# Another order of the products where the up projection ends and the down projection begins

## The chip, the cores and the metric

One core of a Trainium2 chip runs the whole layer in one launch. TensorE (PE in the profile) multiplies, with its weight loads as a row of their own (PEld); VectorE (DVE), ScalarE (ACT) and GpSimd (POOL) do the rest; SyncE (SP) and POOL issue the DMAs. The time is that of the device in microseconds (us), the median of several runs. One run was taken with the hardware profiler, and all rows come from it.

## The reference

A hybrid encoder layer on 512 tokens of width 2048, cut to its steps:

```python
# per layer (DEPTH = 1), x: 512 x 2048 float32
h = rms_norm(x, pre_mix_g);  z = h @ w_in            # q, k, v, u
a = chunked_attention(q, k, v, rel_bias)
p = multiscale_pool(u, pool_w, pool_scale)
x = x + rms_norm(concat(a, p) @ w_o, post_mix_g)
h = rms_norm(x, pre_ffn_g)
up = causal_dwconv(h @ w_up, conv_w, conv_b)         # 512 x 11264, three taps and a bias
y = (gelu(up[:, :5632]) * up[:, 5632:]) @ w_down     # 5632 -> 2048
out = x + rms_norm(y, post_ffn_g)
```

What the change touches is the join of the last two products, `h @ w_up` (2048 to 2 x 5632) and the one with `w_down` (5632 to 2048).

## The kernel before

All numbers are float32. Each factor of a product is split into a high part, rounded by ScalarE (L135), and a low part, the rest, by VectorE (L136); `mm3` makes a product of three matmuls, high by high (L153), high by low (L154) and low by high (L155). So each factor costs a ScalarE and a VectorE pass before TensorE can use it, and TensorE meets the high parts first.

Both projections are multiplied in blocks by Winograd's form of Strassen's scheme: seven products of half-size blocks instead of eight, numbered 1 to 7, with sums of blocks as factors and sums of products as results.

**Up projection.** `w_up` is cut into 22 units of 2 x 256 columns; unit u has a gate member and a product member. The first three units (`PLAIN`) are multiplied plainly; the other 19 make 38 members k = 0 to 37, two to a unit, the even one the gate, the odd one the product. Member k has seven products (k, i), each of 24 matmuls `q<-...` with 256 columns. `Factors.order` is the hand-written order of them all; each get of a factor makes the split four products ahead (`AHEAD`), on four pairs of buffers (`w4`), and raw blocks are loaded up to ten ahead (`RAW`). In the ordinary member the order is 4, 1, 2, then 6 of the member before, 5, 7, then 3 of the member before. Block sums of weights are made by accumulating DMAs on POOL's queue (`add`, L997) in the raw buffer that the product before has left: x holds the factor of 4, then of 5, then of 6, and with VectorE's L1003 that of 3; y holds that of 1, then of 7. In a member that is `alone` the factor of 4 has a raw buffer of its own (`w`), and 5 comes first.

The stationary factors of products 4, 7 and 6 are h4, h7 and h6 (`hs`), high and low, in the right-hand buffers raw1, wh and wl; those buffers later hold the first factors of the down projection.

After (k, 6) `keep_six` sums four of the results (L1045 on ScalarE, L1046 to L1051 on VectorE); after (k, 3) `keep_all` adds the rest (L1056), scales (L1057), and then either `gate` (three taps on ScalarE L846 and VectorE L847, L848, and the gelu L860) or `product` (the same taps, two multiplications L867, and a store to `gd` by POOL, L870 or L872).

**Down projection.** Five chunks c of four units each (the last two units come at the end). In a chunk there are seven products for each of two halves of the columns, cc = 0 and 1: (cc, i). Each has 24 matmuls `p<-bh,ah` and so on with 512 columns, made by `multiply`. The left factor `a` comes from `gd` (`gc` in the trace, loaded at L1140), the right one `t` or `b` from `w_down` (L802, L770); in chunk 0 all sums of right blocks are in DRAM already, so each right factor is one load of 1 MB. `ORDER0` is the order of chunk 0. `keep_product` brings a result from PSUM into a `part` buffer, by ScalarE's copy (L832), or, for products 2, 3 and 4 (`ADDED`), by VectorE's addition to the part of product 1, 5 or 7 (L828), in place; POOL stores it to one of the sums in DRAM, or accumulates it there (L837, L839). There are five `part` buffers.

**The passage.** The buffers of the up projection (`big`, `p3`) are closed before those of the down projection (`p4`) open in the same memory. So the first two products of chunk 0 are prepared while the up projection still runs (`next_first`, `first_left`, `rights`), in old buffers, and multiplied right after its last product; the next ones use buffers of p4, whose loads wait until their memory is free. In what follows P1 to P6 are the first six products of chunk 0.

TensorE's order is that of the code (`manual_schedule`). The instructions of all other engines are put in order by a planner from its own estimate of times, the earlier in the code the sooner where it has the choice; on the chip each engine keeps that order. `issue_after` holds P1's and P2's copies behind the splits of P3.

Of the kernel before, what the change touches and what calls it, by code (L numbers as in the profile page):

```python
# [31 lines left out]
CU = 4  # L32
# [13 lines left out]
def f32(ap):  # L46
    return ap.bitcast(F32)
# [28 lines left out]
def encoder_layer(ctx: ExitStack, tc: tile.TileContext, x, xT, vecs, rel, post_mix, post_ffn,  # L76
# [7 lines left out]
    nc = tc.nc  # L84
# [16 lines left out]
    def bank(name):  # L101
        return psum.tile([P, 512], F32, tag="ps", name=name)
# [4 lines left out]
    def raw4(name):  # L107
        return big.tile([P, 1024], F32, tag="raw", bufs=5, name=name)

    def w4(name):  # L110
        return big.tile([P, 1024], F32R, tag="w4", bufs=8, name=name)
# [21 lines left out]
    def split(hi, lo, src, scale=None):  # L133
        if scale is None:
            rounded = nc.scalar.activation(hi, src, AF.Copy)  # L135
            nc.vector.tensor_sub(lo, src, f32(hi))  # L136
        else:
            rounded = nc.scalar.activation(hi, src, AF.Copy, scale=scale)
            nc.vector.scalar_tensor_tensor(lo, src, scale, f32(hi), op0=ALU.mult, op1=ALU.subtract)
        split.last = rounded.ins  # L140
        return rounded.ins
# [23 lines left out]
    def part(w, *idx):  # L165
        return tuple(v[(slice(None),) + idx] for v in w)
# [24 lines left out]
    def qk_specs(h):  # L191
        return halves(f"q{h}", w_in, head_cols("q", h), 8, P), halves(f"k{h}", w_in, head_cols("k", h), 8, P)
# [24 lines left out]
    for h in range(1, HEADS):  # L217
        q, k = qk_specs(h)
# [67 lines left out]
    for kb in range(KD):  # L286
        i, o = divmod(kb, 8)
        nc.sync.dma_start(xt[kb // 4][:, kb % 4, :], xT[kb * P:(kb + 1) * P, :])
        for what in "qk":
            if kb in chunks:  # L290
                raw, hi, lo = first[f"{what}0_{i}"]
# [5 lines left out]
        for what in "qk":  # L297
            _, hi, lo = first[f"{what}0_{i}"]
# [11 lines left out]
    with tc.tile_pool(name="p1", bufs=2, reuse_waits="tile") as p1:  # L310
# [5 lines left out]
        with tc.issue_after(last_split):  # L316
            for kb in range(KD):
                sq = t512("tmp")
                nc.scalar.activation(sq, xt[kb // 4][:, kb % 4, :], AF.Square)
                if kb == 0:  # L320
                    before = sq
                else:
                    nc.gpsimd.tensor_add(ssum, sq, before)
                    before = ssum
# [419 lines left out]
    gd = [[dram.tile([P, CU, 2, H], F32, name=f"gd{c}_{i}") for i in range(2)] for c in range(NC)]  # L744
# [6 lines left out]
    later, turns = {}, {}  # L751

    def right_tile(tag, name, dt=F32R):

        n = turns[tag] = turns.get(tag, -1) + 1
        if later and n % (2 + LATER[tag]) >= 2:
            return later[tag](name, dt)
        return pr.tile([P, CU, S], dt, tag=tag, bufs=2, name=name)
# [3 lines left out]
    def raw1(name, dt=F32):  # L762
        return right_tile("raw1", name, dt)

    def right(c, cc):

        def load(j, l):
            b = later["raw2"](f"b{j}{l}") if j else raw1(f"b{j}{l}")
            r, cs = 256 * CU * c, slice(l * C + cc * S, l * C + (cc + 1) * S)
            nc.sync.dma_start(b, w_down[r:r + 256 * CU, cs].rearrange(  # L770
                "(u j p) n -> p u j n", j=2, p=P)[:, :, j, :])
            return b

        b = {}
        order = yield
        while True:
            i = order
            if c == 0:

                v = first_right(cc, i, raw1 if ORDER0.index((cc, i)) % 5 < 3 else later["raw2"])  # L780
            else:
                for jl in {1: (11, 12), 7: (22,), 2: (21,)}.get(i, ()):
                    b[jl] = load(jl // 10 - 1, jl % 10 - 1)
                if i == 5:
                    nc.vector.tensor_add(b[11], b[11], b[12])  # L785
                if i == 7:
                    nc.vector.tensor_add(b[12], b[22], b[12])
                if i == 6:
                    nc.vector.tensor_add(b[11], b[11], b[22])
                if i == 4:  # L790
                    nc.vector.tensor_add(b[21], b[21], b[11])
                v = b[{1: 11, 5: 11, 7: 12, 6: 11, 2: 21, 3: 22, 4: 21}[i]]
            hi, lo = right_tile("wh", "bh"), right_tile("wl", "bl")
            split(hi, lo, v)
            order = yield hi, lo

    def first_right(cc, i, ring):

        v = ring(f"t{i}")
        source = first_sum[i][cc] if i in first_sum else first_block(cc, *{1: (0, 0), 2: (1, 0), 3: (1, 1)}[i])  # L800
        with tc.issue_after(first_right.last) if first_right.last else nullcontext():
            first_right.last = nc.sync.dma_start(v, source).ins  # L802
        return v
# [4 lines left out]

    LAST = 1, 2, 5, 7, 6, 3, 4

    ORDER0 = ((0, 1), (0, 2), (1, 1), (1, 2), *((cc, i) for i in (5, 6, 3, 7, 4) for cc in range(2)))
    DEST = {1: "16", 5: "57", 7: "57", 6: "16", 2: "11", 3: "53", 4: "74"}
    ADDED = {2: 1, 3: 5, 4: 7}
    kept, begun = {}, set()

    def multiply(l, r):
        ps = [bank(f"p{t}") for t in range(2)]
        for u in range(CU):
            for t in range(2):
                mm3(ps[t], part(l, u, slice(t * P, (t + 1) * P)), part(r, u), u == 0, u == CU - 1)  # L820
        return ps

    def keep_product(c, cc, i, ps):

        if i in ADDED:
            v = kept.pop((cc, ADDED[i]))
            for t in range(2):
                nc.vector.tensor_add(v[:, t, :], ps[t], v[:, t, :])  # L828
        else:
            v = later["part"]("part")  # L830
            for t in range(2):
                nc.scalar.activation(v[:, t, :], ps[t], AF.Copy)  # L832
            kept[cc, i] = v
        n = DEST[i]
        dest = sums[n][:, cc * S:(cc + 1) * S].rearrange("(t p) n -> p t n", p=P)
        if (n, cc) in begun:
            nc.gpsimd.dma_start(dest, v, accum_op=ALU.add)  # L837
        else:
            nc.gpsimd.dma_start(dest, v)  # L839
            begun.add((n, cc))  # L840

    with tc.tile_pool(name="p3", bufs=2, reuse_waits="tile") as p3:
# [116 lines left out]
        class Factors:  # L959
# [3 lines left out]
            def __init__(self):  # L963
                n = 2 * (NU - PLAIN)

                self.order = []
                for k in range(n):
                    late = [(k - 1, 6), (k - 1, 3)] if k else [None] * 2
                    if k in (0, n - 1):
                        o = [(k, 5), (k, 4), (k, 1), (k, 2), late[0], (k, 7), late[1]]  # L970
                    else:
                        o = [(k, 4), (k, 1), (k, 2), late[0], (k, 5), (k, 7), late[1]]
                    self.order += [v for v in o if v]
                self.order += [(n - 1, 6), (n - 1, 3)]
                self.alone = 0, n - 1
                self.raw, self.made, self.loaded, self.used = {}, [], 0, 0

            def block(self, k, m, kh):
# [49 lines left out]
        factors = Factors()  # L1028
# [41 lines left out]

        def first_left():

            def load(i, j):
                v = raw4(f"a{i}{j}").rearrange("p (u n) -> p u n", u=CU)
                nc.sync.dma_start(v, gd[0][i][:, :, j, :])
                return v

            def parts(v):
                hi, lo = (w4(f"a{p}").rearrange("p (u n) -> p u n", u=CU) for p in "hl")
                split(hi, lo, v)  # L1080
                return hi, lo

            for j in range(2):
                yield parts(load(0, j))

        z = up(1, 0, [spread2, lambda: product(0, gate(0, normed(ups[0])), normed(ups[1]))])
        a = gate(1, normed(z))
# [3 lines left out]
        a = gate(2, normed(z))  # L1091
        z = up(2, 1)
        h_difference()
        product(2, a, normed(z))
        rights, lefts, firsts = [right(0, cc) for cc in range(2)], first_left(), []
        for r in rights:
            next(r)
        end = factors.alone[1]

        def next_first():  # L1100

            _, i = ORDER0[len(firsts)]
            r = rights[0].send(i)
            firsts.append((i, next(lefts), r))

        for k, i in factors.order:
            seven(k, i)
            if (k, i) == (end - 1, 3):
                next_first()
            if i == 6:  # L1110
                keep_six(k)
                if k == end:
                    next_first()
            if i == 3:
                keep_all(k)
        firsts = [(i, multiply(l, r)) for i, l, r in firsts]
    phase.close()

    with tc.tile_pool(name="p4", bufs=2, reuse_waits="tile") as p4:
# [46 lines left out]
        def factors():  # L1166
            nonlocal right_split
            for c in range(NC):
# [7 lines left out]
                order = [(cc, i) for cc, o in ((0, ORDER), (1, LAST if c == NC - 1 else ORDER)) for i in o]  # L1176
                for cc, i in order if c else ORDER0[2:]:
                    r = rs[cc].send(i)
# [11 lines left out]
        for f in factors():  # L1190
            ready.append(f)
            if firsts:
                with tc.issue_after(right_split), tc.issue_after(split.last):
                    for i, ps in firsts:
                        keep_product(0, 0, i, ps)
                firsts = ()
            if len(ready) > AHEAD:
                next_product()
# [54 lines left out]
        parts, scaled, ssqs, befores = [[] for _ in range(NT)], [[] for _ in range(NT)], {}, {}  # L1253
# [110 lines left out]
```

## Time and profile before

| what | us |
|---|---|
| median of 3 runs | 1932.14 (1931.54 to 1932.59) |
| the profiled run's own time | 1932.79 |
| its span, first to last instruction | 1931.0 |
| mean granted TensorE clock | 0.996 |

The up projection ends at 1484.95 us of the span, and P1 begins there. How rows are read: "start, duration, engine, line, operation, out<-in" in a timeline, with the idle time before it and what ended that in brackets; in a table of stretches the busy time of each engine, the granted clock, the DMA engines' busy share and GB/s. Buffer numbers are left out of names, so `bl<-t,bh` is any right factor's low part.

### The profile page before, as it was taken

Reading aid. Unit: us, or ns where it says so; the run is one execution under the profiler, and the core shown is the slowest. Engines: PE = TensorE matmul, PEld = TensorE weight load, DVE = VectorE, ACT = ScalarE, POOL = GpSimd, SP = SyncE. Lnnn points to the kernel's source line nnn. Section 1 sums busy time; section 2 is a strip of 40 time slices with the busy share of each in tenths; the row PEclk is TensorE's granted clock in tenths of the full one; section 3 lists DMA queues with packets and bytes.
Section 4 is the critical chain, followed back from the end, with each engine's and each line's share of the span. In section 5 each row is a group of like instructions: output and inputs, shape, how many; then the busy total and the mean of one; then the engine's idle time right before and its main releaser. Section 6 shows DMA issues by size and latency. Waiting matters only on the chain.

```text
span 1931.0 us, 28650 instructions
## 1 busy us (share of the span) xinstructions
PE 1899.8 (98%) x11566; PEld 1707.9 (88%) x11566; DVE 1432.8 (74%) x1618; ACT 915.5 (47%) x1126; POOL 285.3 (15%) x369
## 2 busy tenths in 40 slices
PE   9999999999979999999999999999999899999998
PEld 7888888888868889999999999999999688888886
DVE  5455345587668756887878878788788799998877
ACT  6333233356445434544544445444454655455543
POOL 5110010000010101111111111111110112222221
PEclk9999999999999999999999999999999999999999
DMA  7598395447695957667676676766766999999997
GB/s 244 162 259 217 120 264 142 133 148 250 188 305 184 287 144 162 155 170 188 150 188 157 168 188 150 186 161 166 188 162 196 324 265 250 255 210 240 227 222 238
DMA packets 182789, 386.90 MB, mean 200 GB/s; under 512 B 10944, under 2 KB 62528, under 8 KB 178624
## 3 DMA queue, kind: packets, MB, share of 16 engines
q1 hardware_dynamic: 132704, 249.79, 38.0%
q0 software_dynamic: 49952, 135.28, 37.1%
q8 instruction: 90, 1.47, 0.3%
q14 instruction: 43, 0.35, 0.1%
HBM read 328.40 MB, written 98.57 MB: 221 GB/s over the span
## 4 chain that ended last, share of the span: by engine, by line
PE 92%; DMA 3%; issue 2%; DVE 1%; ACT 1%; SPq 0%; POOL 0%; POOLq 0%; DVEq 0%; ACTq 0%
PE q L154 14%; PE q L153 14%; PE q L155 14%; PE p L155 6%; PE p L153 6%; PE p L154 6%; PE up L154 2%; PE up L155 2%; PE up L153 2%; PE m L153 2%; PE m L154 2%; PE m L155 2%; PE u L153 2%; PE v L153 2%; PE u L154 2%
## 5 line engine op out<-in xcount | busy, mean ns | idle before, releaser
L154 PE MATMUL q<-gTl,wfh 128*128 128x256 f32 x1216 | 344.1, 283 | 0.0
L155 PE MATMUL q<-gTh,wfl 128*128 128x256 f32 x1216 | 344.1, 283 | 0.0
L153 PE MATMUL q<-gTh,wfh 128*128 128x256 f32 x1216 | 344.1, 283 | 0.0
L153 PEld LDWEIGHTS q<-gTh,wfh 128*128 128x128 f32 x1216 | 233.5, 192 | 0.0
L154 PEld LDWEIGHTS q<-gTl,wfh 128*128 128x128 f32 x1216 | 233.5, 192 | 0.0
L155 PEld LDWEIGHTS q<-gTh,wfl 128*128 128x128 f32 x1216 | 233.5, 192 | 0.0
L153 PE MATMUL p<-bh,ah 128*128 128x512 f32 x560 | 219.3, 392 | 4.5 <-ACT ah L135 4.5
L154 PE MATMUL p<-bl,ah 128*128 128x512 f32 x560 | 219.1, 391 | 2.3 <-DVE bl L136 2.3
L155 PE MATMUL p<-bh,al 128*128 128x512 f32 x560 | 219.5, 392 | 1.7 <-DVE al L136 1.7
L135 ACT ACTIVATE wfh<-wx 128x1024 fp32r<-128x1024 f32 x152 | 159.9, 1056 | 119.1 <-PE q L154 91.4
L136 DVE TENSOR_TENSOR wfl<-wx,wfh 128x1024 fp32r<-128x1024 f32 x152 | 183.9, 1220 | 33.5 <-ACT wfh L135 33.4
L135 ACT ACTIVATE wfh<-wy 128x1024 fp32r<-128x1024 f32 x76 | 80.6, 1061 | 119.3 <-PE q L154 105.8
L135 ACT ACTIVATE bh<-b 128x2048 fp32r<-128x2048 f32 x56 | 106.9, 1917 | 61.3 <-DVE b L785 40.6
L136 DVE TENSOR_TENSOR bl<-b,bh 128x2048 fp32r<-128x2048 f32 x56 | 127.7, 2287 | 10.5 <-PE p L154 8.5
L153 PEld LDWEIGHTS p<-bh,ah 128*128 128x128 f32 x560 | 105.8, 189 | 27.1 <-ACT ah L135 5.3
L155 PEld LDWEIGHTS p<-bh,al 128*128 128x128 f32 x560 | 105.9, 189 | 24.8 <-DVE al L136 2.9
L997 POOL DMA_DIRECT2D wx<-in_w_up x76 | 67.5, 888 | 408.3 <-DVE wfl L136 381.5
L154 PEld LDWEIGHTS p<-bl,ah 128*128 128x128 f32 x560 | 105.8, 189 | 24.8 <-DVE bl L136 2.6
L136 DVE TENSOR_TENSOR wfl<-wy,wfh 128x1024 fp32r<-128x1024 f32 x76 | 92.9, 1223 | 32.2 <-ACT wfh L135 30.9
L837 POOL DMA_DIRECT2D sum<-part x60 | 72.7, 1231 | 251.4 <-DVE part L828 109.3
L136 DVE TENSOR_TENSOR wfl<-wz,wfh 128x1024 fp32r<-128x1024 f32 x38 | 46.6, 1225 | 59.7 <-ACT wfh L135 59.7
L153 PE MATMUL q<-h4h,wfh 128*128 128x256 f32 x304 | 86.0, 283 | 0.0
(590 smaller groups left out, 4953.7 us busy)
## 6 DMA issues: line engine op xcount, KB each, us to landing
wx<-in_w_up POOLq DMA_DIRECT2D x76, 512.0 KB, 7.0
sum<-part POOLq DMA_DIRECT2D x70, 512.0 KB, 8.2
b<-in_w_down SPq DMA_DIRECT2D x32, 1024.0 KB, 8.9
wx<-in_w_up SPq DMA_DIRECT2D x40, 512.0 KB, 6.1
wy<-in_w_up SPq DMA_DIRECT2D x38, 512.0 KB, 5.5
wz<-in_w_up SPq DMA_DIRECT2D x38, 512.0 KB, 7.0
wy<-in_w_up POOLq DMA_DIRECT2D x38, 512.0 KB, 7.4
wt<-in_w_o POOLq DMA_DIRECT2D x12, 1024.0 KB, 12.2
```

What stands on the lines that cost most here:

```text
L135: rounded = nc.scalar.activation(hi, src, AF.Copy)
L136: nc.vector.tensor_sub(lo, src, f32(hi))
L153: nc.tensor.matmul(ps, l[0], r[0], start=first, stop=False)
L154: nc.tensor.matmul(ps, l[0], r[1], start=False, stop=False)
L155: nc.tensor.matmul(ps, l[1], r[0], start=False, stop=last)
L837: nc.gpsimd.dma_start(dest, v, accum_op=ALU.add)
L997: nc.gpsimd.dma_start(self.raw[k, what], self.block(k, m, kh), accum_op=ALU.add)
```

## The change

Four things are set otherwise.

- In `Factors.order` member 36 is `alone` too, and (36,6) and (36,3) stand at the head of member 37, whose own products follow as 1, 5, 4, 2, 7, 6, 3. So member 36, the gate of the last unit, is finished when seven products are left, and these are all of the last member.
- `ORDER0` begins with (0,1), (1,1), (0,2), (1,2) instead of (0,1), (0,2), (1,1), (1,2). P1 and P2 are product 1 of both column halves.
- `first_left` loads and splits one left half only, which P1 and P2 share; it is prepared after (37,7), and P2's right factor after (37,6), as before.
- The sum of (0,2), VectorE's L828, writes a `part` buffer of its own instead of the one of (0,1). That of (1,2) stays in place, and so do all others.

```diff
--- before.py
+++ after.py
@@ -808,7 +808,7 @@
 
     LAST = 1, 2, 5, 7, 6, 3, 4
 
-    ORDER0 = ((0, 1), (0, 2), (1, 1), (1, 2), *((cc, i) for i in (5, 6, 3, 7, 4) for cc in range(2)))
+    ORDER0 = ((0, 1), (1, 1), (0, 2), (1, 2), *((cc, i) for i in (5, 6, 3, 7, 4) for cc in range(2)))
     DEST = {1: "16", 5: "57", 7: "57", 6: "16", 2: "11", 3: "53", 4: "74"}
     ADDED = {2: 1, 3: 5, 4: 7}
     kept, begun = {}, set()
@@ -823,9 +823,12 @@
     def keep_product(c, cc, i, ps):
 
         if i in ADDED:
-            v = kept.pop((cc, ADDED[i]))
+            v = before = kept.pop((cc, ADDED[i]))
+            if (c, i) == (0, 2):
+
+                v = later["part"]("part")
             for t in range(2):
-                nc.vector.tensor_add(v[:, t, :], ps[t], v[:, t, :])
+                nc.vector.tensor_add(v[:, t, :], ps[t], before[:, t, :])
         else:
             v = later["part"]("part")
             for t in range(2):
@@ -963,16 +966,18 @@
             def __init__(self):
                 n = 2 * (NU - PLAIN)
 
+
+                self.alone = 0, n - 2, n - 1
                 self.order = []
                 for k in range(n):
                     late = [(k - 1, 6), (k - 1, 3)] if k else [None] * 2
-                    if k in (0, n - 1):
+                    if k == n - 1:
+                        o = [*late, (k, 1), (k, 5), (k, 4), (k, 2), (k, 7), (k, 6), (k, 3)]
+                    elif k in self.alone:
                         o = [(k, 5), (k, 4), (k, 1), (k, 2), late[0], (k, 7), late[1]]
                     else:
                         o = [(k, 4), (k, 1), (k, 2), late[0], (k, 5), (k, 7), late[1]]
                     self.order += [v for v in o if v]
-                self.order += [(n - 1, 6), (n - 1, 3)]
-                self.alone = 0, n - 1
                 self.raw, self.made, self.loaded, self.used = {}, [], 0, 0
 
             def block(self, k, m, kh):
@@ -1070,18 +1075,11 @@
 
         def first_left():
 
-            def load(i, j):
-                v = raw4(f"a{i}{j}").rearrange("p (u n) -> p u n", u=CU)
-                nc.sync.dma_start(v, gd[0][i][:, :, j, :])
-                return v
-
-            def parts(v):
-                hi, lo = (w4(f"a{p}").rearrange("p (u n) -> p u n", u=CU) for p in "hl")
-                split(hi, lo, v)
-                return hi, lo
-
-            for j in range(2):
-                yield parts(load(0, j))
+            v = raw4("a").rearrange("p (u n) -> p u n", u=CU)
+            nc.sync.dma_start(v, gd[0][0][:, :, 0, :])
+            hi, lo = (w4(f"a{p}").rearrange("p (u n) -> p u n", u=CU) for p in "hl")
+            split(hi, lo, v)
+            return hi, lo
 
         z = up(1, 0, [spread2, lambda: product(0, gate(0, normed(ups[0])), normed(ups[1]))])
         a = gate(1, normed(z))
@@ -1092,20 +1090,20 @@
         z = up(2, 1)
         h_difference()
         product(2, a, normed(z))
-        rights, lefts, firsts = [right(0, cc) for cc in range(2)], first_left(), []
+        rights, firsts = [right(0, cc) for cc in range(2)], []
         for r in rights:
             next(r)
-        end = factors.alone[1]
+        end = factors.alone[-1]
 
         def next_first():
 
-            _, i = ORDER0[len(firsts)]
-            r = rights[0].send(i)
-            firsts.append((i, next(lefts), r))
+            cc, i = ORDER0[len(firsts)]
+            r = rights[cc].send(i)
+            firsts.append((firsts[0][0] if firsts else first_left(), r))
 
         for k, i in factors.order:
             seven(k, i)
-            if (k, i) == (end - 1, 3):
+            if (k, i) == (end, 7):
                 next_first()
             if i == 6:
                 keep_six(k)
@@ -1113,7 +1111,7 @@
                     next_first()
             if i == 3:
                 keep_all(k)
-        firsts = [(i, multiply(l, r)) for i, l, r in firsts]
+        firsts = [multiply(l, r) for l, r in firsts]
     phase.close()
 
     with tc.tile_pool(name="p4", bufs=2, reuse_waits="tile") as p4:
@@ -1191,8 +1189,8 @@
             ready.append(f)
             if firsts:
                 with tc.issue_after(right_split), tc.issue_after(split.last):
-                    for i, ps in firsts:
-                        keep_product(0, 0, i, ps)
+                    for cc, ps in enumerate(firsts):
+                        keep_product(0, cc, 1, ps)
                 firsts = ()
             if len(ready) > AHEAD:
                 next_product()
```

## The prediction

> **What bounds the kernel now.** I read the page first, then the stretches around the passage, TensorE's timeline there, and VectorE's timeline for what TensorE waited for.
>
> ```profile
> span 1931.0 us, 28650 instructions
> PE 1899.8 (98%) x11566; PEld 1707.9 (88%) x11566; DVE 1432.8 (74%) x1618; ACT 915.5 (47%) x1126; POOL 285.3 (15%) x369
> PE 92%; DMA 3%; issue 2%; DVE 1%; ACT 1%; SPq 0%; POOL 0%; POOLq 0%; DVEq 0%; ACTq 0%
> ```
>
> TensorE is the bound: 98% busy and 92% of the chain. The change leaves its matmuls as they are, 24 to a product, so it can win only where TensorE stands idle or runs at a lower clock. By stretches (PE, PEld, DVE, ACT, POOL busy, then granted clock, DMA share, GB/s):
>
> ```profile
> 1484.00:1498.00 14.00, 12.32 (x58) 9.71 (x56) 12.98 (x17) 5.15 (x5) 0.00 (x0) 1.00 0.95 341
> 1498.00:1504.00 6.00, 2.87 (x6) 1.86 (x7) 6.00 (x6) 5.69 (x6) 1.26 (x2) 0.82 1.01 367
> 1514.00:1523.00 9.00, 5.38 (x16) 3.75 (x15) 8.14 (x7) 4.66 (x3) 0.60 (x1) 0.81 0.69 235
> 1600.00:1800.00 200.00, 200.00 (x884) 165.62 (x883) 184.51 (x122) 107.83 (x96) 44.73 (x37) 1.00 1.00 241
> ```
>
> Two holes with the clock at 0.82 and 0.81, then 200 us without one. In TensorE's timeline of the passage the last q matmuls, the first two down products (P1, P2) and the three after them (P3 to P5) show each loss:
>
> ```profile
> 1484.71 0.28 PE L154 MATMUL q<-gTl,wfh 128*128 128x256 f32 x1
> ...
> 1484.95 0.40 PE L153 MATMUL p<-bh,ah 128*128 128x512 f32 x1
> ...
> 1490.65 0.39 PE L154 MATMUL p<-bl,ah 128*128 128x512 f32 x1
> 1491.54 0.50 PE L155 MATMUL p<-bh,al 128*128 128x512 f32 x1 [0.50 <-DVE al L136]
> 1491.87 0.40 PE L153 MATMUL p<-bh,ah 128*128 128x512 f32 x1
> ...
> 1496.43 0.39 PE L155 MATMUL p<-bh,al 128*128 128x512 f32 x1
> 1498.23 0.51 PE L153 MATMUL p<-bh,ah 128*128 128x512 f32 x1 [1.42 <-ACT ah L135]
> 1501.00 0.50 PE L154 MATMUL p<-bl,ah 128*128 128x512 f32 x1 [2.26 <-DVE bl L136]
> 1502.13 0.79 PE L155 MATMUL p<-bh,al 128*128 128x512 f32 x1 [0.64 <-DVE al L136]
> 1502.72 0.63 PE L153 MATMUL p<-bh,ah 128*128 128x512 f32 x1
> ...
> 1505.51 0.40 PE L154 MATMUL p<-bl,ah 128*128 128x512 f32 x1
> ...
> 1513.91 0.39 PE L155 MATMUL p<-bh,al 128*128 128x512 f32 x1
> 1517.35 0.50 PE L153 MATMUL p<-bh,ah 128*128 128x512 f32 x1 [3.05 <-ACT ah L135]
> ...
> 1522.40 0.40 PE L155 MATMUL p<-bh,al 128*128 128x512 f32 x1
> ```
>
> Undisturbed pace: 37 steps lie between 1505.51 and 1513.91, so 8.40/37 = 0.227 us a matmul and 5.45 us a product. Against it:
> - P2's start: two steps from 1490.65 to 1491.87, 1.22 - 0.45 = **0.77 lost**, for the low part of the second left factor.
> - P3's start: 11 steps from 1496.43 to 1505.51, 9.08 - 2.50 = **6.58 lost**. Of this 1.20 is clock: the seven steps from 1502.72 to 1505.51 took 2.79 where 1.59 is the pace.
> - P5's start: 12 steps from 1513.91 to 1522.40, 8.49 - 2.72 = **5.77 lost**, clock included.
>
> Together 13.1 us (0.68%): all that this change can win. Why P3 and P5 were late stands in VectorE's timeline, an engine that works in its order:
>
> ```profile
> 1482.29 2.28 DVE L136 TENSOR_TENSOR bl<-t,bh 128x2048 fp32r<-128x2048 f32 x1
> 1484.49 1.41 DVE L847 SCALAR_TENSOR_TENSOR ca<-z,vec,ca 128x511 f32<-128x511 f32 x2
> 1485.81 1.41 DVE L848 SCALAR_TENSOR_TENSOR ca<-z,vec,ca 128x510 f32<-128x510 f32 x2
> 1487.13 0.42 DVE L1046 TENSOR_TENSOR z<-q,z 128x256 f32<-128x256 f32 x1
> ...
> 1490.27 1.21 DVE L136 TENSOR_TENSOR al<-a,ah 128x1024 fp32r<-128x1024 f32 x1
> 1491.40 0.42 DVE L1050 TENSOR_TENSOR z<-q,z 128x256 f32<-128x256 f32 x1
> ...
> 1498.66 2.28 DVE L136 TENSOR_TENSOR bl<-t,bh 128x2048 fp32r<-128x2048 f32 x1
> 1500.86 2.35 DVE L136 TENSOR_TENSOR al<-gc,ah 128x1024 fp32r<-128x1024 f32 x2
> 1503.13 2.28 DVE L136 TENSOR_TENSOR bl<-t,bh 128x2048 fp32r<-128x2048 f32 x1
> 1511.58 1.29 DVE L828 TENSOR_TENSOR part<-p,part 128x512 f32<-128x512 f32 x2 [6.17 <-DMA sum<-part]
> ```
>
> P3 waits because the taps of gate 21 (`ca`), a second left split (`al<-a`) and the last pair's own work stand ahead of `bl` and `al` at 1498.66 and 1500.86. P5 waits because the sum L828 of product (0,2) is made in place in a buffer whose store is still on its way; for 6.17 us VectorE does nothing, and P5's `bl`, `s` and `al` are queued behind it:
>
> ```profile
> 1499.84 11.65 DMA sum<-part
> ```
>
> **The change, part by part.**
>
> *Member 36 finished when seven q products are left.* The count of q products is the same. Gate 21's taps leave the passage: from 1484.49 to 1487.13, 2.64 us off VectorE's queue ahead of P3. They go among the last seven q products. In the stretch of the last nine it has this much to do already (DVE alone in the first row; then the stretch before, and a row of the page on DMA issues):
>
> ```profile
> 1458.00:1482.00 24.00, 20.00 (x24) 1.00 0.47 132
> ...
> 1440.00:1460.00 20.00, 20.00 (x169) 20.00 (x169) 15.63 (x19) 10.17 (x13) 2.56 (x3) 1.00 0.57 127
> ...
> wx<-in_w_up SPq DMA_DIRECT2D x40, 512.0 KB, 6.1
> ```
>
> With them 22.6 of 24 us. Cover: the weight splits run four products ahead on four buffer pairs, so each has three products to be made in, 3 x 24 x 0.12 = 8.6 us (0.12 a q step: 1484.71 to 1484.95 is two). I cost it at nothing; without that cover, each us that a split is late is a us. Member 36 now loads its i=4 block apart from its i=5 sum: one `wx` load more on SP's queue (512 KB, 6.1 us), issued some ten products ahead where the DMA share is about 0.57; POOL's accumulating adds stay as many, the first of them issued at the load instead of behind a split. Hidden by those ten products: nothing. In the last member (37,5) and (37,6) now stand four products apart instead of seven, and between them lie a split and one add of such a block, about 1.2 + 6.1 inside 4 x 2.88 = 11.5 us.
>
> *First right loads later.* The two `t` buffers lie on h4's, which (37,4) frees. That product moves from eight places before the end to five, so the loads go from 1464.87 to 1484.95 - 4 x 2.88 = 1473.4. Their landings, and ScalarE's split:
>
> ```profile
> 1464.87 19.09 SPq L802 DMA_DIRECT2D t<-in_w_down  x3
> DMA to landing us min/median/max: 5.8/7.6/10.5
> 1495.34 1.90 ACT L135 ACTIVATE bh<-t 128x2048 fp32r<-128x2048 f32 x1
> ```
>
> By the ends 5.8 and 10.5 they land at 1479.2 and 1483.9. P1's `bl` can start only when (37,6) has freed h6, at 1482.1, in both kernels (1482.29 above); so P1 starts on time. P2's right is split by 1483.9 + 1.9 + 2.28 = 1488.1, due at 1490.4. Cost nothing, margin 2.3.
>
> *One left half for both first products.* A load, a ScalarE split and a VectorE split go before P2, and the same in P3/P4 (there one of the two `al`). P2's 0.77 goes to nothing. From VectorE's queue ahead of P3 go 1490.27 to 1491.40, 1.13 us. A load on SP's queue waited for that split, and goes out sooner, the later ones with it:
>
> ```profile
> SPq L802 <- DVE al L136: 5.7, 1, 5.7
> ```
>
> *P3.* Its `al`, first of the two at 1500.86, ended at about 1502.03. Less 2.64 and 1.13 that is 1498.26. Due: P1's first matmul plus 50 steps, 1484.95 + 11.35 = 1496.30. So 1.96 stays lost. Bounds: nothing, if the planner puts `bl` and `al` ahead of product 21's taps, and 6.58 as before. For the clock I take the 1.20 of before in full, because the row nearest to such a wait (2.26) was followed by it; its ends are 0 and 1.20. P3's loss: 3.2 instead of 6.58.
>
> [...]
>
> *P2's sum in an own buffer.* L828 of (0,2), now P3's, reads (0,1)'s part and writes another; it waits for no store. VectorE after `al` at 1498.3: two `bl` (4.4, by starts 2.2 each), `s`, `al` and L828 (about 1.2 each by the `al` and L828 rows) end at about 1506.3; P5 is due at 1484.95 + 4 x 5.45 + 3.2 = 1509.9. Lost 0 of 5.77; bounds 0 and 5.77. The wait that takes its place is L828 of (1,2), still in place, in (1,1)'s part. That store can leave when P2 has ended, about 1496.3 with 1 or 2 us for the copies, and with the 11.65 above lands at 1509 to 1510. P4's sum is due when P4 ends, also about 1510. So it waits little, and behind it stands `bl` of P6 with 5.45 us to spare. One part buffer of five more is held for a while; nothing.
>
> *Sum.* 13.1 - 3.2 = 9.9 us less. The profiled run took 1932.79 and would take 1922.9; it lies 0.65 above the median of the runs, so the median goes from 1932.14 to **1922.3**. About 0.2% (3.9 us) is what a measurement of this kernel can tell from no change.
>
> **The rivals.**
>
> *Half of it stays.* Either P3 keeps all its loss (the planner, which orders every engine but TensorE, fills the room with other work): 1932.14 - 0.77 - 5.77 = 1925.6. Or L828 of (1,2) waits for its store as (0,2)'s did, and 5.77 moves on to a later product: 1928.0 with P3 as forecast. For it: the loads that now go out sooner share the way with these stores. [...] Against: P4's sum comes 5.45 us after the one that waited.
>
> *Given back.* Past the passage VectorE is 184.51 of 200 us busy and the DMA share is 1.00; were one of them the bound, being there sooner would win nothing: 1932. Against: TensorE is busy 200.00 of 200 there.
>
> *Slower: the first right loads come too late.* Place: P1's start. `bh` and `bl` need 4.2 us, so with X from issue to landing P1 starts at 1473.4 + X + 4.2, and each us of X over 7.3 is one of TensorE's. It eats the 9.9 at X = 16 to 17 (1.2 for the clock); at X = 21 it is 13.7 + 1.2 - 9.9 = 5.0 slower, 1937.1. For: loads a little later do take so long:
>
> ```profile
> DMA to landing us min/median/max: 7.4/12.1/15.4
> ```
>
> Against: those stood in a queue of four at 0.95 to 1.01 DMA share; at 1473 it is near empty, and the loads of before took 5.8 and 10.5 beside a store.
>
> **How the numbers follow.** Forecast 0.58, half stays 0.22, given back 0.10, slower 0.10. All 13.1 gone is 1919.0, the low end. The high end, 1930.0, takes in P3 unchanged and part of the store's wait together; beyond it lie "slower" and most of "given back", under 0.2. Faster by over 0.2% (below 1928.3): 0.58 and nearly all of the 0.22, 0.78. Within: 0.12. Slower: 0.10.
>
> **What would show it.** Right: no wait of L828 for a store over 1 us; P5 starts with no hole and clock 1.00 behind it; a hole at P3 of 1 to 3 us, ended by `bl` or `al`; no wait in the q products; P1 at 0.12 behind the last q matmul. Wrong: a hole at P1 ended by `bh` or `bl`, TensorE waiting for `wfl` in the last nine q products, L828 of (1,2) with VectorE idle for several us, or holes after 1523 that were not there.

## The result, and the profile after

The changed kernel takes **1924.09 us** (median of 5 runs, 1923.17 to 1924.78) against 1932.14 for the kernel before (again the median, of 5 runs beside it, 1931.42 to 1933.00): a ratio of 0.9958, interval 0.9943 to 0.9972. The forecast was 1922.3. The profiled runs went from 1932.79 to 1924.09. In the page of the kernel after, the span and the busy times read:

```profile
span 1922.3 us, 28647 instructions
PE 1898.8 (99%) x11566; PEld 1708.8 (89%) x11566; DVE 1429.2 (74%) x1616; ACT 913.0 (47%) x1124; POOL 285.3 (15%) x369
```

TensorE's matmuls are as many as before and its busy time is 1.0 us shorter; the span is 8.7 us shorter. So what went is nearly all idle time. The table of stretches of the kernel after (PE, PEld, DVE, ACT, POOL busy, granted clock, DMA share, GB/s) shows where:

```profile
1458.00:1482.00 24.00, 24.00 (x203) 24.00 (x202) 23.16 (x29) 14.34 (x17) 2.27 (x3) 1.00 0.58 154
...
1498.00:1504.00 6.00, 5.70 (x18) 4.52 (x19) 2.54 (x2) 2.15 (x2) 0.00 (x0) 0.72 1.00 399
...
1514.00:1523.00 9.00, 9.00 (x41) 7.46 (x40) 9.00 (x8) 6.94 (x8) 1.42 (x2) 1.00 1.00 371
```

In 1514 to 1523, where TensorE was busy for 5.38 of 9 us, it is now busy throughout. In 1498 to 1504 it is busy for 5.70 of 6 us, but the clock stands at 0.72: a busy TensorE is not a fast one there. TensorE's timeline of the kernel after, at the starts of P1, P3 and P5:

```profile
1484.72 0.28 PE L155 MATMUL q<-gTh,wfl 128*128 128x256 f32 x1
1484.84 0.40 PE L153 MATMUL p<-bh,ah 128*128 128x512 f32 x1
...
1495.75 0.39 PE L153 MATMUL p<-bh,ah 128*128 128x512 f32 x1
1497.16 0.50 PE L154 MATMUL p<-bl,ah 128*128 128x512 f32 x1 [1.03 <-DVE bl L136]
1498.30 0.50 PE L155 MATMUL p<-bh,al 128*128 128x512 f32 x1 [0.64 <-DVE al L136]
...
1499.35 0.52 PE L153 MATMUL p<-bh,ah 128*128 128x512 f32 x1
...
1503.00 0.40 PE L153 MATMUL p<-bh,ah 128*128 128x512 f32 x1
...
1511.53 0.50 PE L155 MATMUL p<-bh,al 128*128 128x512 f32 x1 [0.42 <-DVE al L136]
```

Against the pace of 0.227 us a matmul: P2 loses nothing. At P3 the two steps into 1497.16 and 1498.30 lose 1.41 - 0.23 and 1.14 - 0.23, 2.1 us; the nine steps from 1499.35 to 1503.00 took 3.65 where 2.04 is the pace, 1.6 us of half clock; P3 in all 3.83. P5 loses 0.68. So the loss at the passage went from 13.1 to 4.5 us, and from the first down matmul to the last it is 385.19 us instead of 393.77: 8.58 less. That is the whole gain; P1 starts 0.11 us earlier, and what follows the last down matmul takes 52.3 us in both.

VectorE's timeline of the kernel after shows what still comes late (lines have moved: L831 is the sum that was L828, L870 the multiplication that was L867):

```profile
1493.62 1.29 DVE L870 TENSOR_TENSOR ca<-ca,cb 128x512 f32<-128x512 f32 x2
1494.82 2.29 DVE L136 TENSOR_TENSOR bl<-t,bh 128x2048 fp32r<-128x2048 f32 x1
1497.02 1.22 DVE L136 TENSOR_TENSOR al<-gc,ah 128x1024 fp32r<-128x1024 f32 x1
...
1504.57 0.69 DVE L831 TENSOR_TENSOR part<-p,part 128x512 f32<-128x512 f32 x1 [3.90 <-PE p L155]
1505.18 2.28 DVE L136 TENSOR_TENSOR bl<-t,bh 128x2048 fp32r<-128x2048 f32 x1
1507.38 1.22 DVE L1150 TENSOR_TENSOR s<-gc 128x1024 f32<-128x1024 f32 x1
1510.25 1.22 DVE L136 TENSOR_TENSOR al<-s,ah 128x1024 fp32r<-128x1024 f32 x1
```

P3's `bl` and `al` stand behind the last product's taps and multiplications, of which L870 is the last. And where VectorE waited 6.17 us for a store, it now waits 3.90 us for P3 itself: the planner put the first half of the sum of (0,2) ahead of `bl`, `s` and `al` of P5, and P5's `al` comes at 1511.5, 0.42 us late.

### The profile page after: what moved, and what is told of

The parts are those of the page before. It is cut to its first block, busy times and chain, and to the rows that moved or that the text cites. A ratio compares the mean times of both kernels' runs of the same rounds, so it can differ in the third digit from the quotient of the medians.

```text
span 1922.3 us, 28647 instructions
## 1 busy us (share of the span) xinstructions
PE 1898.8 (99%) x11566; PEld 1708.8 (89%) x11566; DVE 1429.2 (74%) x1616; ACT 913.0 (47%) x1124; POOL 285.3 (15%) x369
## 4 chain that ended last, share of the span: by engine, by line
PE 90%; DVE 3%; DMA 3%; ACT 2%; issue 1%; SPq 0%; POOL 0%; POOLq 0%; DVEq 0%; ACTq 0%
PE q L154 14%; PE q L155 14%; PE q L153 14%; PE p L155 6%; PE p L154 6%; PE p L153 6%; PE up L154 2%; PE up L153 2%; PE up L155 2%; PE m L154 2%; PE m L153 2%; PE m L155 2%; PE u L155 2%; PE v L155 2%; PE u L153 2%; PE v L153 2%
## 5 line engine op out<-in xcount | busy, mean ns | idle before, releaser
L155 PE MATMUL q<-h6h,wfl 128*128 128x256 f32 x304 | 86.1, 283 | 0.0
```

The costliest lines, as they stand in the source:

```text
L155: nc.tensor.matmul(ps, l[1], r[0], start=False, stop=last)
```

## The experiments

Two theories. **Two losses:** the sum that waits for its store (P5) and the queue of VectorE ahead of P3 are separate, and each part of the change removes its own. **One loss:** one part does it all, P5 being late only because P3 was (or the reverse). "Lost" is TensorE's time over the pace at the product named, to about 0.1 us, half clock included; "p" is from the first to the last down matmul. Both are of the one profiled run. P1's own start lies between 1484.8 and 1486.3 us in these profiles, which is settled ahead of the passage, so p is what tells the kernels apart; the medians go with it. Each ratio is to the kernel before as it was timed beside that variant (medians 1931.79 to 1933.14), so medians of different rows are compared only as closely as that.

| kernel | median | ratio to before (interval) | lost P2 / P3 / P5 | p |
|---|---|---|---|---|
| before | 1932.14 | | 0.77 / 6.58 / 5.77 | 393.77 |
| after | 1924.09 | 0.9958 (0.9943 to 0.9972) | 0 / 3.83 / 0.68 | 385.19 |
| own_only | 1927.87 | 0.9976 (0.9965 to 0.9986) | 0.8 / 7.1 / 0 | 388.55 |
| after_in_place | 1930.24 | 0.9989 (0.9980 to 0.9998) | 0 / 2.21 / 7.3 | 390.11 |
| q_order_only | 1930.33 | 0.9984 (0.9975 to 0.9993) | 0 / 4.85 / 6.3 | 391.73 |
| down_only | 1927.71 | 0.9972 (0.9962 to 0.9982) | 0 / 7.3 / 0.7 | 388.65 |
| after_again | 1924.47 | 0.9955 (0.9943 to 0.9967) | 0 / 4.31 / 0.68 | 385.73 |
| pool_mul | 1926.42 | 0.9962 (0.9950 to 0.9974) | 0 / 4.85 / 0.7 | 386.19 |
| late_sum | 1923.44 | 0.9950 (0.9938 to 0.9962) | 0 / 2.21 / 0 | 382.85 |
| both | 1922.49 | 0.9952 (0.9938 to 0.9966) | 0 / 1.55 / 0; 0.1 in P1 | 382.27 |
| passes_p3 | 1921.16 | 0.9940 (0.9927 to 0.9952) | 0 / 0.21 / 1.14; 0.2 in P1 | 382.21 |
| passes_all | 1927.79 | 0.9973 (0.9964 to 0.9982) | 0 / 0.34 / 0; 6.4 later | 387.49 |
| before_passes | 1940.46 | 1.0041 (1.0027 to 1.0055) | 0 / 3.39 / 9.68; 7.6 later | 401.51 |
| passes_late | 1919.60 | 0.9936 (0.9922 to 0.9949) | 0 / 0 / 0 | 380.60 |

### own_only: before, with own buffers for the sums of product 2

```diff
-            v = kept.pop((cc, ADDED[i]))
+            v = before = kept.pop((cc, ADDED[i]))
+            if (c, i) == (0, 2):
+                v = later["part"]("part")
...
-                nc.vector.tensor_add(v[:, t, :], ps[t], v[:, t, :])
+                nc.vector.tensor_add(v[:, t, :], ps[t], before[:, t, :])
```

> Before, with the one edit that product 2's sums of chunk 0 go to part buffers of their own. Theory (two separate losses: VectorE's queue ahead of P3, and the in-place sum that waits for its store ahead of P5): the wait of 6.17 us at L828 and P5's hole go, P3's hole of 6.6 stays; 5.8 us less than before, 1926.4. Rival (one loss: the late P3 is the cause, and the wait for the store lies in time that is lost anyway): at most 2 us less, 1930 or more.

P5's loss fell from 5.77 us to nothing and P3's stayed (7.1 against 6.58, the difference being half clock); p is 5.2 us shorter. In VectorE's timeline of this kernel the sum (L830 here) runs at once when P3's `al` is made, with no idle time before it:

```profile
1502.60 1.28 DVE L830 TENSOR_TENSOR part<-p,part 128x512 f32<-128x512 f32 x2
```

So P5 was late for the store alone; P3's lateness doesn't pass on to it.

### after_in_place: after, with these sums in place again

```diff
             v = before = kept.pop((cc, ADDED[i]))
-            if (c, i) == (0, 2):
-
-                v = later["part"]("part")
```

> After, with product 2's sums in place again. Theory: L831 of (0,2) waits for the store of (0,1), which landed at 1508.4 in the profile of after, instead of starting at 1504.6; VectorE stands for some 4 us more with P5's bl, s and al behind it, so P5 is late by about as much: 1928. Rival (one loss): no change within 1 us of after, 1924.

The wait is back, in VectorE's and TensorE's timelines of this kernel:

```profile
1509.46 0.69 DVE L828 TENSOR_TENSOR part<-p,part 128x512 f32<-128x512 f32 x1 [7.34 <-DMA sum<-part]
```

```profile
1498.62 0.50 PE L154 MATMUL p<-bl,ah 128*128 128x512 f32 x1 [1.03 <-DVE bl L136]
1499.75 0.50 PE L155 MATMUL p<-bh,al 128*128 128x512 f32 x1 [0.63 <-DVE al L136]
...
1514.63 0.79 PE L153 MATMUL p<-bh,ah 128*128 128x512 f32 x1 [4.18 <-ACT ah L135]
```

P5 loses 7.3 us and p is 4.9 longer than after's (some 4 was expected). The new order without the own buffer is worth little: the sum comes earlier, the store does not come earlier by as much, and what P3 won is mostly waited away at P5. P3 has the holes of after to 0.01 us, yet it lost 2.21 and not 3.83: the clock stayed at 1.00.

### q_order_only and down_only: the two orders apart

q_order_only is before with the new order of the q products:

```diff
+                self.alone = 0, n - 2, n - 1
...
-        end = factors.alone[1]
+        end = factors.alone[-1]
...
-            if (k, i) == (end - 1, 3):
+            if (k, i) == (end, 7):
```

> Before, with the new order of the q products alone; P1 and P2 stay products 1 and 2 of the first column half, with two left halves and the sum in place. Theory: gate 21's taps leave VectorE's queue, 2.6 us off P3, and P5's wait stays: 1929.5. Rival (one loss, cured by the order): nearly all of the gain of after, 1925 to 1926.

down_only is after with the old order of the q products, so it has the shared left half, the new `ORDER0` and the own buffers:

```diff
-                self.alone = 0, n - 2, n - 1
...
-            if (k, i) == (end, 7):
+            if (k, i) == (end - 1, 3):
```

> After, with the old order of the q products: the new order of chunk 0, the shared left half and the own buffers alone. Theory: 5.8 for P5, 0.8 for P2's start and 1.1 of the split ahead of P3: 7.7 us less than before, about 1924.5, so that the q order would be worth little on top. Rival (one loss, cured by the q order): 1930.

In TensorE's timeline of q_order_only the hole at P3 shrinks, and P5 waits as in before:

```profile
1499.03 0.50 PE L154 MATMUL p<-bl,ah 128*128 128x512 f32 x1 [2.04 <-DVE bl L136]
...
1515.30 0.79 PE L153 MATMUL p<-bh,ah 128*128 128x512 f32 x1 [2.81 <-ACT ah L135]
```

In down_only P5 is cured (the table) and P3 isn't; its timeline of TensorE there:

```profile
1499.96 0.79 PE L154 MATMUL p<-bl,ah 128*128 128x512 f32 x1 [2.26 <-DVE bl L136]
```

P3's 2.26 is that of before to the digit, yet the saved split did come. VectorE's and TensorE's rows in down_only, the second as stretches:

```profile
1497.62 2.29 DVE L136 TENSOR_TENSOR bl<-t,bh 128x2048 fp32r<-128x2048 f32 x1
```

```profile
1499.41:1502.83 3.42, 2.52 (x5) 1.73 (x6) 3.42 (x3) 3.27 (x2) 0.84 (x2) 0.50 1.00 398
1502.83:1506.24 3.41, 3.41 (x9) 2.63 (x9) 0.42 (x1) 0.00 (x0) 0.00 (x0) 0.50 1.00 419
```

P3's `bl` starts 1.04 us sooner than before's (1498.66), and P3's first matmul 1.03 sooner (1497.20 against 1498.23), so the hole between them is as long as it was. But the half clock lasted 6.83 us here and 3.41 at P3 in before, which costs about 1 us more, and P2's 0.77 only made P3 due sooner. So P2 and P3 together lose 7.3 us as in before. This forecast is a miss: 7.7 us were expected, p is 5.1 shorter; the rest is the 0.8 of P2, counted though P3 waits for VectorE all the same, the 1 us of clock, and 0.7 that stays at P5. With the gate's taps away too (q_order_only against after), the saved split shows in P3's loss: 4.85 against 3.83 and 4.31, with 3.41 us of half clock in each. The theory of two losses stands; that of one falls. The terms don't add to what the whole change won: q order alone won 2.0 us of p, and without an own buffer the store takes back part of what P3 wins; own buffers alone won 5.2; all together 8.6.

### after_again: the changed kernel once more

> After once more, beside the three variants of it on the same chip. Theory: 8 us less than before, holes of about 2 us at P3 and 0.7 at P5; the half clock behind P3's hole may be there or not (the profile of after had it, that of after_in_place with the same hole had not), 1.7 us of difference.

P5's loss is the same 0.68, and the clock falls again. The half clock at the passage lasted 3.41 us in before (each of two times), in after and in after_again, and 6.83 in down_only. The tables in stretches of 3.41 us, counted from a start of a half clock in each profile (after, after_again, and after_in_place, whose holes at P3 are as long as after's):

```profile
1496.06:1499.48 3.42, 1.76 (x7) 1.18 (x7) 3.29 (x3) 3.42 (x3) 1.39 (x2) 1.00 1.02 398
1499.48:1502.89 3.41, 3.41 (x10) 2.62 (x9) 1.19 (x1) 0.67 (x1) 0.00 (x0) 0.50 1.00 413
```

```profile
1495.82:1499.24 3.42, 1.26 (x5) 0.56 (x4) 3.42 (x3) 3.42 (x5) 1.97 (x3) 1.00 1.02 410
1499.24:1502.65 3.41, 3.41 (x10) 2.66 (x9) 1.72 (x1) 1.15 (x1) 0.00 (x0) 0.50 0.97 399
```

```profile
1495.71:1499.12 3.41, 2.38 (x10) 1.41 (x8) 3.41 (x4) 3.33 (x6) 1.98 (x3) 1.00 1.01 425
1499.12:1502.53 3.41, 2.78 (x13) 2.35 (x13) 2.87 (x2) 2.48 (x2) 0.00 (x0) 1.00 1.00 368
```

In after both holes lie in one stretch, TensorE is busy for 1.76 us of it, and the next stretch is at 0.50; so it is in after_again, with 1.26. In after_in_place the same holes as in after are divided between two stretches, 2.38 and 2.78 us busy, and the clock stays at 1.00. So the length of the holes does not settle the half clock. What differs is how they lie in these stretches; that this is the cause was not shown.

### pool_mul: the last product's multiplications on GpSimd

```diff
-                nc.vector.tensor_mul(g[:, j, :], g[:, j, :], c)
+                (nc.gpsimd if u == NU - 1 else nc.vector).tensor_mul(g[:, j, :], g[:, j, :], c)
```

> After, with the two multiplications of the last product member (L870, 1.29 us of VectorE ahead of P3's bl and al) given to GpSimd. Theory (P3 waits for VectorE's queue and nothing else): bl and al end 1.2 us sooner, P3's hole falls from 2.1 us to under 1, and no half clock follows: 1.2 to 3 us less than after, 1921 to 1923. Rival (P3's rest is set by the landing of its loads or by ScalarE, or GpSimd slows VectorE): no gain.

A miss. VectorE's queue is 1.29 us shorter ahead of P3, and P3 loses no less: 4.85 against 4.31. The timelines of GpSimd and VectorE in this kernel:

```profile
1494.51 4.96 POOL L870 TENSOR_TENSOR ca<-ca,cb 128x512 f32<-128x512 f32 x2 [24.68 <-issue]
```

```profile
1494.94 3.39 DVE L136 TENSOR_TENSOR bl<-t,bh 128x2048 fp32r<-128x2048 f32 x1
1498.26 2.30 DVE L136 TENSOR_TENSOR al<-gc,ah 128x1024 fp32r<-128x1024 f32 x1
```

`bl` took 3.39 instead of 2.29 and `al` 2.30 instead of 1.22: 2.2 us more, beside two multiplications on GpSimd. That pair ran from 1494.51 to 1499.47, `bl` and `al` from 1494.94 to 1500.56.

### late_sum: the sum of (0,2) behind P5's splits

```diff
+            split.low = nc.vector.tensor_sub(lo, src, f32(hi)).ins
...
                         made[i] = ls.send(i)
+                        left_low[c, i] = split.low
...
-            keep_product(c, cc, i, multiply(l, r))
+            ps = multiply(l, r)
+            with tc.issue_after(left_low[0, 5]) if (c, cc, i) == (0, 0, 2) else nullcontext():
+                keep_product(c, cc, i, ps)
```

> After, with VectorE's sum of (0,2) held behind the low split of P5's left factor. Theory (P5's 0.7 us comes from VectorE standing 3.9 us at that sum for P3's end with P5's splits behind it): P5's hole goes, 0.7 us less than after, which its timeline shows and the time hardly. Rival (P5 waits for its load or for ScalarE): the hole stays.

VectorE's timeline of this kernel, and the stretch at P3:

```profile
1498.97 4.50 DVE L136 TENSOR_TENSOR bl<-t,bh 128x2048 fp32r<-128x2048 f32 x2
...
1505.78 1.22 DVE L136 TENSOR_TENSOR al<-s,ah 128x1024 fp32r<-128x1024 f32 x1
1506.91 0.68 DVE L831 TENSOR_TENSOR part<-p,part 128x512 f32<-128x512 f32 x1
```

```profile
1498.00:1504.00 6.00, 5.37 (x23) 4.24 (x23) 5.87 (x4) 2.75 (x2) 0.15 (x1) 1.00 1.01 408
```

P5's `al` is made 4.5 us earlier and the hole is gone: P5's loss in after was the place of the sum in VectorE's queue. The holes at P3 are 1.03 and 0.63 us again, at clock 1.00, and P3 loses 2.21. The medians of late_sum and after_again differ by 1.0 us with overlapping intervals, so as a time this loss isn't shown; as a hole it is.

### both: pool_mul and late_sum together

> After with both: GpSimd's multiplications and the sum held back. Theory: the gains add, 2 to 3.7 us less than after, 1920.5 to 1922. Rival: what one wins the other loses, because VectorE, ahead by then, waits elsewhere: no better than the better one of the two.

It can't be told from late_sum alone (1922.49 and 1923.44, intervals overlapping). P3's holes are 0.34 and 0.63, so `bl` came sooner here; the price is on GpSimd, whose two multiplications take 8.37 us (4.96 in pool_mul; beside them `bl` and `al`, from 1494.60 and 1496.81 on, keep their usual 2.29 and 1.22), and on the two `bl` from 1499.10 on, 5.59 instead of 4.50:

```profile
1494.17 8.37 POOL L870 TENSOR_TENSOR ca<-ca,cb 128x512 f32<-128x512 f32 x2 [24.66 <-issue]
```

```profile
1499.10 5.59 DVE L136 TENSOR_TENSOR bl<-t,bh 128x2048 fp32r<-128x2048 f32 x2 [1.07 <-ACT bh L135]
```

### passes_p3, passes_all, before_passes: high parts first

A product's 24 matmuls are three kinds mixed, so the second of them needs `bl` and the third `al`. Here they come in three passes of eight, high by high first; the low parts are due 8 and 16 matmuls later. In passes_p3 (from after) that is done for P3 alone, in passes_all (from after) for all down products, in before_passes for all of them in the kernel before.

```diff
+        for k, (a, b) in enumerate(((0, 0), (0, 1), (1, 0)) if passes else ()):
+            for u in range(CU):
+                for t in range(2):
+                    nc.tensor.matmul(ps[t], part(l, u, ...)[a], part(r, u)[b],
+                                     start=k == u == 0, stop=k == 2 and u == CU - 1)
```

> After, with P3's 24 matmuls in three passes: the eight high by high first, then the eight that need bl, then the eight that need al. Same matmuls. Theory (what is left at P3 is only that bl and al come 1.0 and 2.1 us after bh and ah, out of VectorE's queue): the first pass takes 1.8 us and the second 1.8, which covers both; P3's hole and the half clock behind it go, 2.2 to 4.3 us less than after_again, 1920 to 1922; P5's 0.7 stays. Rival (P3's high parts are as late, or the new order of weight loads costs TensorE): no gain.

TensorE's timeline of passes_p3, and the stretch:

```profile
1495.98 1.98 PE L821 MATMUL p<-bh,ah 128*128 128x512 f32 x8
1497.89 2.12 PE L821 MATMUL p<-bl,ah 128*128 128x512 f32 x8
1499.85 1.98 PE L821 MATMUL p<-bh,al 128*128 128x512 f32 x8
...
1508.58 0.50 PE L155 MATMUL p<-bh,al 128*128 128x512 f32 x1 [0.87 <-DVE al L136]
```

```profile
1498.00:1504.00 6.00, 6.00 (x27) 4.95 (x28) 5.54 (x4) 2.62 (x2) 0.19 (x1) 1.00 1.01 401
```

P3 has no hole and the clock stays at 1.00, with VectorE's queue as it was. That shows that P3's remaining loss was the lateness of the two low parts, with the half clock that followed it. P5 loses 1.14 for the sum ahead of its splits.

> After, with every down product in three passes. Theory: as passes_p3, and P5's hole, which al ends, goes too: 0.7 us less than passes_p3, 1919.5 to 1921.5, with TensorE's pace of 227 ns a matmul unchanged. Rival: the order costs TensorE in each of 70 products; at 3 ns a matmul that would be 5 us more.

The passage is clean here, and the pace within a product is the same 0.227 us, but 6.4 us are lost further on, which neither theory nor rival had expected. The timelines of TensorE and ScalarE in passes_all at the larger hole:

```profile
1654.69 3.60 PE L821 MATMUL p<-bh,ah 128*128 128x512 f32 x8 [2.82 <-ACT bh L135]
```

```profile
1651.78 1.06 ACT L135 ACTIVATE ah<-gc 128x1024 fp32r<-128x1024 f32 x1 [6.62 <-DMA gc<-gd]
1652.74 3.69 ACT L135 ACTIVATE bh<-b 128x2048 fp32r<-128x2048 f32 x2
```

ScalarE stood 6.62 us for the load of a left block, and the `bh` that TensorE needed was queued behind it. Why that load comes later with passes was not followed; it stays open.

> Before, with every down product in three passes. Theory: P3's high left part came 1.4 us late there by itself and bl 2.3 us after it, so of P3's 6.6 us the first 1.4 and part of the second stay; P5's ah is 3.05 us late and is not helped: 2 to 4 us less than before, 1929 to 1931, so the passes do not do what the change does. Rival (the order of the passes alone would have been enough): 1925 or less.

Slower than before, where 2 to 4 us less was expected. P3's loss halved, to 3.39, and P5's rose by more, to 9.68: TensorE comes to P5 sooner and waits there for the same store. TensorE's and VectorE's timelines of this kernel (L833 is the sum):

```profile
1517.86 2.50 PE L821 MATMUL p<-bh,ah 128*128 128x512 f32 x5 [7.58 <-ACT ah L135]
```

```profile
1512.09 1.29 DVE L833 TENSOR_TENSOR part<-p,part 128x512 f32<-128x512 f32 x2 [6.76 <-DMA sum<-part]
```

In before P5 began at 1517.35 and its sum at 1511.58. So without an own buffer the store, not TensorE, sets the start of P5. The other 7.6 us are lost later, with the open cause of passes_all.

### passes_late: passes for P3, and the sum behind P5's splits

The edits of passes_p3 and late_sum together.

> passes_p3 with the sum of (0,2) held behind the low split of P5's left factor, as in late_sum: both of the holes that the change leaves are treated. Theory: P5's hole of 1.1 us goes and nothing comes in its place, about 1 us less than passes_p3, 1920; all of the passage's 13.1 us would then be won but some tenths. Rival: VectorE's order, moved by the planner, opens a hole elsewhere: 1921 or more.

1919.60 us (1918.96 to 1920.21), 0.9936 of before (0.9922 to 0.9949). The median is the lowest here, but as a ratio it can't be told from passes_p3 (0.9940, 0.9927 to 0.9952); p, 380.60 against 382.21, shows the difference. Its table of stretches:

```profile
1498.00:1504.00 6.00, 6.00 (x28) 4.99 (x27) 5.86 (x4) 2.36 (x2) 0.00 (x0) 1.00 1.00 398
1504.00:1514.00 10.00, 10.00 (x46) 8.28 (x45) 9.97 (x9) 7.59 (x6) 0.72 (x1) 1.00 1.02 411
1514.00:1523.00 9.00, 9.00 (x42) 7.44 (x41) 7.24 (x6) 7.25 (x9) 2.14 (x3) 1.00 1.03 429
```

TensorE has no hole left at the passage. 393.77 - 380.60 = 13.2 us from P1 on: the 13.1 that the prediction counted as all there was to win.

## Why the prediction was right, point by point

- **What there was to win, 13.1 us.** Right: passes_late won 13.2 of p, with nothing more lost there.
- **The q products' splits cost nothing.** Right: VectorE is busy for 23.16 of 24 us in 1458 to 1482 (22.6 was worked out), and TensorE for all 24.
- **First right loads.** Right, with room: issued at 1473.4, landed after 5.6 and 7.7 us, where 10.5 was taken and 16 to 17 would have eaten the gain. P1 started 0.12 behind the last q matmul.

```profile
DMA to landing us min/median/max: 5.6/6.7/7.7
```

- **P2's 0.77.** Right: nothing lost. The shared left half was not needed for it: with the new order of the q products alone, and two left halves, P2 loses nothing either (q_order_only).
- **P3's `al`.** Forecast to end at 1498.26; 1497.02 + 1.22 is 1498.24. The hole is 2.2 us by late_sum and after_in_place, where 1.96 was forecast. So the queue was counted rightly: 2.64 of taps and 1.13 of a split went from it. P3's first hole in before, 1.42 us for ScalarE's `ah`, came from the same queue: ahead of that `ah` ScalarE's L846 had waited 5.53 us for VectorE's L1057. In after that `ah` is made 1.4 us before P3 begins.
- **The clock term was mis-sized.** 1.20 was taken whole; it is 1.6 in after, and 0 with the same holes in after_in_place and late_sum. The step took it from the size of the hole ("the row nearest to such a wait (2.26) was followed by it"), which does not settle it: 0.50 for 3.41 us in after, 1.00 with the same holes in the other two. The rows before could not tell that, so it was luck that the term came near.
- **P5's loss of 0 was the other miss.** 0.68 was left. The step counted VectorE's work behind `al` as one sum, ending at 1506.3, and never asked for its order: L831 stood ahead of P5's `bl`, waited 3.90 us for P3's end, and the rest came after. late_sum shows it. The list also left out a subtraction ahead of that `al` (L1157, 1.22 us); with it the sum would end at 1507.5, still before 1509.9.
- **A misreading of the change.** The text says that the sum of (1,2) stays in place, and looks for a new wait there. The code's condition names chunk and product, not the half, so both halves got an own buffer, two `part` buffers more and not one, and that wait could not arise. Since it was costed at near nothing, the sum did not move; the rival built on it (1928.0) had no ground.
- **The sum.** 9.9 was forecast, 8.6 came from P1 on: 0.4 for the clock, 0.2 for P3's holes and 0.7 for P5. The 1.8 us between 1922.3 and 1924.09 are about this 1.3, less the 0.1 that P1 starts sooner, and 0.65 that was subtracted since the profiled run before lay above its median; the profiled run after lies on its own.
- **The rivals.** Half stays by P3: it did not, though P3 kept 3.83. That loads and stores share the way shows in the profile before: in 1498 to 1514 the loads' queue (q1) took 75.8% of the 16 engines' time and the stores' (q0) 16.0%. Given back: no, TensorE has no hole after 1523. Slower by late loads: no.

## What to carry to other kernels

Write down, product by product, when each factor is due and which instructions stand ahead of it in its engine's queue; a sum of durations without their order misses a wait in the middle. The sum made in place waited for the store of what it overwrites, 6.17 us in before and 7.34 in after_in_place, and everything queued behind it waited too, so that time won ahead of it was lost again: give such a sum its own buffer before tuning what comes earlier. Where only the low parts were late, multiplying the high parts first hid them (P3 lost 0.21 us in passes_p3, 3.83 in after); do it at that one place and not everywhere (1921.16 against 1927.79 here).

## What the runs showed of the hardware that was not expected

**A half clock came behind some holes and not behind others of the same length.** Holes of 1.03 and 0.64 us with a matmul between were followed by 3.41 us at clock 0.50 in after, which cost 1.6 us, and holes of 1.03 and 0.63 by clock 1.00 in after_in_place and late_sum; in after_again, after a hole of 1.53 us and another of 0.63, the clock fell to 0.50 again. In the profiles of before and after, the end of the kernel left aside, a clock of 0.50 begins six times:

| profile | from (us) | for (us) | TensorE busy in the 3.41 us before |
|---|---|---|---|
| before | 570.01 | 3.41 | 0.87 |
| before | 1501.85 | 3.41 | 0.80 |
| before | 1518.92 | 3.41 | 1.00 |
| after | 567.64 | 6.83 | 0.92 |
| after | 594.95 | 3.41 | 1.54 |
| after | 1499.48 | 3.41 | 1.76 |

The starts lie 273 and 5 times 3.413 us apart in before, 8 and 265 times in after. Stretches cut at the same steps with TensorE busy for 1.60 to 1.68 us (before from 576.84 and from 590.49, after from 574.47 and from 1912.49) were at 1.00 and followed by 1.00. So the busy time ahead does not settle it alone either; what does was not shown.

**VectorE's splits took longer beside multiplications on GpSimd, but not all of them.** Beside the pair on GpSimd in pool_mul (4.96 us), VectorE's `bl` took 3.39 us instead of 2.29 and `al` 2.30 instead of 1.22. In the run both the pair took 8.37 us from 1494.17 on; beside it `bl` and `al` took 2.29 and 1.22, and the next two `bl` 5.59 together instead of 4.50 (the profile's spans on GpSimd are rough). What these multiplications take on GpSimd with VectorE idle was not measured, nor why one pair took longer than the other.
